# RWKV stage of a hybrid trunk: key transposes in another PSUM ring, the y split on another engine, a denser inverse

## The chip, the core and the metric

The kernel runs on one core of a Trainium2 chip. The metric is device time in microseconds (us) of one execution; lower is better. TensorE (PE) does the matrix products and transposes, VectorE (DVE), ScalarE (ACT) and GpSimd (POOL) the elementwise work, SyncE (SP) issues most of the transfers. Each engine takes its instructions strictly in order, so one that waits holds up all that stand behind it. TensorE's clock has two levels, 2.4 GHz (granted clock 1.0) and 1.2 GHz (0.5).

## The reference

One layer on 2048 tokens of width 1024. After a modulated RMS norm a projection feeds two halves of width 512, an RWKV-7 recurrence and a banded attention; both are gated, joined and projected out.

```python
def rwkv7_step(state, inp):
    r_t, w_t, k_t, v_t, a_t, b_t = inp
    sa = einsum('bhij,bhj->bhi', state, a_t)
    state = state * w_t + sa[..., None] * b_t + v_t[..., None] * k_t
    y = einsum('bhij,bhj->bhi', state, r_t)
    return state, y
...
y = group_norm(y) * lnx_g + lnx_b + sum(r * k * r_k) * v      # per head of 64
y = concat([y_r * silu(g_r), y_a * silu(g_a)])
x = x + gate * (y @ w_out)
```

## The kernel before

Phase A computes norm, projections and attention. The last stage, `phase_r`, runs the recurrence over 32 chunks of 64 tokens (`n` = 0 to 31), eight heads at once; four chunks make a block (`b` = 0 to 7, `c` = 0 to 3 inside it). Within a chunk the recurrence is a triangular system of 64 steps, so each chunk needs the inverse of a triangular matrix.

One chunk, in program order: `from_state` (products with the carried state `z`), `state_keys(n+1)` (PE turns the next chunk's keys, `ps_kt`, and ACT copies them to `kt`), `solve` (`ps_u`, then `uv`), `merge1` and `merge2` (they join the 32-wide inverses into 64-wide ones: `ps_mg`, `ps_mh`), `state` (`ps_z`; two DVE operations write the next `z`), `read_out` (`ps_py`, then `ys`), `qchunk(b+2)` (`ps_q`; DVE masks it into `g`), `from_values(n+1)`. Every second chunk `values` centres the values of a pair (`vf`, `ps_vr`), and the output of the pair before goes through `spread`, `scaled`, `flip` (transposes, `ps_yf`) and `gated` (two DVE operations on `yf`).

The inverse of a block's 32-wide pieces is DVE work alone: `inv(b+1)` has 31 steps of two operations (`pd`, then `xtt`), run during block `b`. When it is done SP writes it out (`xt_d`), reads it back into `g`, and DVE transposes it (`turn`, tile `x`). Only then can `merge1` of the next block's first chunk start; this stands at the end of the last chunk of a block, and is called the border below.

Between these pieces stands `gap()`: it lets one step of the output projection (`outputs`, three 512-wide products into `ps_out`) run on PE, and as many inverse steps on DVE as a rule on the number of calls asks for. The projection goes through 7 jobs of 32 steps. For its last four steps a job loads the next job's y (`yraw`), and `split_y` cuts it into a high part (`yh`, a cast on ACT) and a rest (`yl`, a subtraction). There is one `yh` and one `yl` tile for each quarter, so a cast waits for the last product that reads the tile.

The order on PE, DVE and ACT is the written one (`PINNED`); POOL and SP are ordered by the compiler's scheduler. Two PSUM rings have two buffers each. `psm` (tag `m`) holds `ps_kt`, `ps_mg`, `ps_vr`, `ps_yf` and `ps_q`; `ps_u` (tag `u`) holds `ps_u`, `ps_z` and `ps_mh`. A tile can be written when the tile two places before it in the ring has been read.

Of the kernel before, what the change touches and what calls it, by code (L numbers as in the profile page):

```python
# [9 lines left out]
F32 = mybir.dt.float32  # L10
# [8 lines left out]
P = 128  # L19
# [6 lines left out]
NP = 4  # L26
# [20 lines left out]
CS = {}  # L47
# [107 lines left out]
def q_setup(tc, nc, e, ra):  # L155
    eyes, pool, dp, C, ar_d, kb_d, y_d = (e[k] for k in ("eyes", "pool", "dp", "C", "ar_d", "kb_d", "y_d"))
    wo, xT, outT, psp, modv, split_half, gemm_k, sub = (e[k] for k in ("wo", "xT", "outT", "psp", "modv", "split_half", "gemm_k", "sub"))
    xa_d = dp.tile([KT, P, S], F32, name="xa_d")
    yr_d = dp.tile([NP, P, S], F32, name="yr_d")
    rq = pool("rq", e["ctx"], bufs=1, side="right", reuse_waits="tile")  # L160
# [97 lines left out]
            nc.gpsimd.dma_start(out=xa_d[m, :, tsl], in_=xt)  # L258
            yield

    return dict(xa_d=xa_d, yr_d=yr_d, y_d=y_d, rq=rq, ra=ra, prefetch=prefetch, st=blk_st, qchunk=qchunk, qmat=qmat, inv=inv, output=output, late=late)


def seq(*gs):
# [524 lines left out]
def phase_r(tc, nc, e, q_):  # L789
    C, col, ident = (e[k] for k in ("C", "col", "ident"))  # L790
    nhalf, pool, wcall, sub, gemm_k = (e[k] for k in ("nhalf", "pool", "wcall", "sub", "gemm_k"))
    bv_d, v_d, sg_d, wo, xT, cst, outT, wx, psp, modv = (e[k] for k in ("bv_d", "v_d", "sg_d", "wo", "xT", "cst", "outT", "wx", "psp", "modv"))
    xa_d, yr_d, y_d, rq, ra, blk_st = (q_[k] for k in ("xa_d", "yr_d", "y_d", "rq", "ra", "st"))
    NB, NCH = S // TR, S // 64
    LO, HI = slice(0, 64), slice(64, 128)
# [2 lines left out]
    with st:  # L798
# [9 lines left out]
        def load_pair(name, src, m):  # L808
            o = rp.tile([P, NP, P], F32, name=name, bufs=1)
            nc.sync.dma_start(out=o, in_=src[:, :, m * P:(m + 1) * P].rearrange("k p t -> p k t"))  # L810
            return o
# [5 lines left out]

        def state_keys(n):
            kb = of(n)[1]
            pk = psm("ps_kt")  # L820
            for p in range(NP):
                nc.tensor.transpose(pk[:, p * P:(p + 1) * P], kb[:, p].rearrange("p a b -> p (a b)"), ident)  # L822
            kts[n] = rp.tile([P, 8, 64], F32, name="kt", bufs=2)
            nc.scalar.copy(out=kts[n].rearrange("p a b -> p (a b)"), in_=pk)

        def values(n):
            vf = vfs.pop(n // 2)
            pv = psm("ps_vr")
            for p in range(NP):
                nc.tensor.matmul(pv[:, p * P:(p + 1) * P], lhsT=vf[:, p], rhs=cen, start=(p == 0), stop=(p == NP - 1))  # L830
            pv = pv.rearrange("p (a b) -> p a b", b=64)
            for d in range(2):
                uvs[n + d] = rp.tile([P, 8, 64], F32, name="uv", bufs=3)
                for q, (hr, _) in enumerate(HALVES):
                    nc.scalar.copy(out=uvs[n + d][hr, q::2, :], in_=pv[64 * d:64 * d + 64, q::2, :])
# [63 lines left out]
        def state(n, z):  # L899
            pz = ps_u.tile([P, NP, 64], F32, name="ps_z", tag="u")  # L900
            for i in range(NP):
                for q, (hr, _) in enumerate(HALVES):
                    nc.tensor.matmul(pz[hr, i, :], lhsT=kts[n][:, 2 * i + q, :], rhs=uvs[n][:, 2 * i + q, :], start=(i == 0), stop=(i == 3))
            zn = rp.tile([P, NP, 64], F32, name="z", tag="z", bufs=2)
            nc.vector.tensor_tensor(out=zn, in0=pz, in1=z, op=ALU.add)
            nc.vector.tensor_tensor(out=zn, in0=zn, in1=wcall[:, :, n].unsqueeze(2).broadcast_to([P, NP, 64]), op=ALU.mult)
            return zn

        def read_out(n, ys):
            g = of(n)[2]  # L910
            yr = slice(64 * (n % 2), 64 * (n % 2) + 64)
            for i in range(NP):
                for q, (hr, _) in enumerate(HALVES):
                    nc.tensor.matmul(pys[n][q][hr, i, :], lhsT=g[:, 2 * i + q, 0:64], rhs=uvs[n][:, 2 * i + q, :],
                                     start=False, stop=(i == 3))
            for q, (hr, _) in enumerate(HALVES):
                nc.scalar.copy(out=ys[yr, q::2, :], in_=pys[n][q][hr])

        def square(ys):
            ysq = rp.tile([P, 8, 64], F32, name="ysq", bufs=1)  # L920
            nc.scalar.activation(ysq, ys, AF.Square)
            return ysq
# [12 lines left out]
        def flip(ys):  # L935
            pf = psm("ps_yf")
            for p in range(NP):
                nc.tensor.transpose(pf[:, p * P:(p + 1) * P], ys[:, 2 * p:2 * p + 2, :].rearrange("p a b -> p (a b)"), ident)
            yf = rp.tile([P, NP, P], F32, name="yf", bufs=2)
            for p in range(NP):  # L940
                nc.scalar.activation(yf[:, p, :], pf[:, p * P:(p + 1) * P], AF.Identity, scale=col("lg", p), bias=col("lb", p))
            return yf
# [36 lines left out]
        def split_y(r, k):  # L979
            n = r.shape[1]  # L980
            hi, lo = (ra.tile([P, 512], F32R, name=f"{t}{k}", bufs=1)[:, 0:n] for t in ("yh", "yl"))
            nc.scalar.copy(out=hi, in_=r)
            sub(nc.gpsimd, lo, r, hi)
            return hi.unsqueeze(1), lo.unsqueeze(1)

        def outputs(jobs, fin):
# [40 lines left out]
        fill = outputs(jobs, False)  # L1027
        work = dict(inv=iter(()), calls=0, done=0)

        def gap():  # L1030
            next(fill, None)
            work["calls"] += 1
            want = min(32, max(0, 9 * (work["calls"] - 4) // 4))
            while work["done"] < want:
                next(work["inv"], None)
                work["done"] += 1

        cen = rp.tile([P, P], F32, name="cen", bufs=1)
        nc.sync.dma_start(out=cen, in_=cst[:, CS["cen"][0]:CS["cen"][1]])
        with tc.manual_schedule(engines=PINNED):  # L1040
            z = rp.tile([P, NP, 64], F32, name="z", tag="z", bufs=2)
            nc.gpsimd.memset(z, 0.0)
            vfs[0] = load_pair("vf", v_d, 0)
            for m in range(2):
                load_w(m, 1)
            load_sides(0)
            turn(0)
            state_keys(0)
            merge1(0)
            values(0)  # L1050
            merge2(0)
            gap()
            from_values(0)
            pend = None
            for n in range(NCH):
                b, c = divmod(n, NCB)
                even, more, border = n % 2 == 0, n + 1 < NCH, n % NCB == NCB - 1
                if c == 0:
                    if b + 2 < NB:
                        q_["prefetch"](b + 2)  # L1060
                    work.update(inv=q_["inv"](b + 1) if b + 1 < NB else iter(()), calls=0, done=0)
                    next(work["inv"], None)
                pb = from_state(n, z)
                if more:
                    state_keys(n + 1)
                gap()
                solve(n, pb)
                if more and not border:
                    merge1(n + 1)
                if even and more:  # L1070
                    vfs[n // 2 + 1] = load_pair("vf", v_d, n // 2 + 1) if n + 2 < NCH else None
                if even and pend is not None:
                    scaled(*pend[1:])
                gap()
                gap()
                yf = None
                if even and pend is not None:
                    yf = flip(pend[1])
                elif not even and more:
                    values(n + 1)  # L1080
                zn = state(n, z)
                if even:
                    ys = rp.tile([P, 8, 64], F32, name="ys", bufs=1)
                read_out(n, ys)
                z = zn
                if not even:
                    ysq = square(ys)
                gap()
                if yf is not None:
                    gated(pend[0], yf)  # L1090
                    load_sides(n // 2)
                gap()
                if more and border:
                    turn(b + 1)
                    merge1(n + 1)
                gap()
                if more:
                    merge2(n + 1)
                if not even:
                    pend = n // 2, ys, spread(ysq)  # L1100
                if b + 2 < NB:
                    q_["qchunk"](b + 2, c, psm)
                if more:
                    from_values(n + 1)
            for _ in range(12):
                next(fill, None)
            scaled(*pend[1:])
            yf = flip(pend[1])
            drain(fill)
            gated(pend[0], yf)  # L1110
            drain(outputs([(3, 0, 256, 256)], True))
# [44 lines left out]
```

## Time and profile before

| | |
|---|---|
| median of three runs | 1775.95 us (1772.7 to 1777.89) |
| profiled execution | 1771.38 us, of which the span is 1769.6 us |
| mean granted clock | 0.951 |
| DMA traffic | 231.6 MB |

The span counts from the first to the last instruction of the program. All times of day below are us from its start. The RWKV stage takes the stretch from about 1265 to 1770.

### The profile page before, as it was taken

To read this page: it belongs to the slowest core of one execution; us is meant where nothing else is said; L and a number is where in the kernel's file an instruction comes from. 1 tells how busy PE (TensorE), PEld (TensorE's weight loads), DVE (VectorE), ACT (ScalarE), POOL (GpSimd) and SP (SyncE) were. 2 spreads that over 40 slices of the span, in tenths; PEclk is the share of its full clock that TensorE was granted. 3 is DMA by queue.
4 is the path that set the end of the run, shared out by engine and by line. 5 is a ranking of instruction groups with operands and counts; after the bars stand their busy time and mean duration, and the time that the engine had idled before them with its cause. 6 is when DMAs were issued, how large, how long until landed. Compare 5 with 4: busy or idle time off the path is not lost. (4 is left out here: it accounts for less than half of the span.)

```text
span 1769.6 us, 32130 instructions
## 1 busy us (share of the span) xinstructions
PE 1553.7 (88%) x11944; PEld 1270.9 (72%) x11944; DVE 1090.2 (62%) x2407; ACT 929.9 (53%) x2087; POOL 708.4 (40%) x571
## 2 busy tenths in 40 slices
PE   3899998899999899999979999978688889889795
PEld 2677876678777678888868878856576667767685
DVE  7647457475576846746566574576555576566732
ACT  3666556566555565656566666652234344444440
POOL 4455544555444455444536544505212121221221
PEclk9999999899999999999999999999788999899897
DMA  8463333332324523223142332255746665664532
GB/s 286 130 222 102 100 114 101 114 119 73 113 93 135 167 72 125 81 93 114 60 137 72 126 102 66 66 192 159 229 129 183 167 195 154 187 183 122 148 115 90
DMA packets 188957, 231.60 MB, mean 131 GB/s; under 512 B 62976, under 2 KB 101632, under 8 KB 188800
## 3 DMA queue, kind: packets, MB, share of 16 engines
q1 hardware_dynamic: 183552, 212.76, 39.6%
q0 software_dynamic: 5248, 16.78, 2.7%
q8 instruction: 94, 1.54, 0.4%
q14 instruction: 63, 0.52, 0.1%
HBM read 171.30 MB, written 58.20 MB: 130 GB/s over the span
## 5 line engine op out<-in xcount | busy, mean ns | idle before, releaser
L111 POOL TENSOR_TENSOR wlo<-raw,whi 128x512 fp32r<-128x512 f32 x272 | 369.9, 1364 | 424.4 <-ACT whi L122 374.9
L122 ACT CAST whi<-raw 128x512 fp32r<-128x512 f32 x272 | 167.6, 618 | 173.9 <-issue 53.5
L130 PE MATMUL ps_r<-hh,whi 128*128 128x512 f32 x544 | 219.5, 404 | 13.8 <-ACT carry L632 10.6
L132 PE MATMUL ps_r<-hh,wlo 128*128 128x512 f32 x544 | 218.1, 401 | 2.2 <-POOL wlo L111 2.2
L131 PE MATMUL ps_r<-hl,whi 128*128 128x512 f32 x544 | 218.1, 401 | 0.0
L130 PE MATMUL ps_qkvg<-hh,whi 128*128 128x512 f32 x480 | 196.0, 410 | 10.7 <-ACT carry L632 7.1
L131 PE MATMUL ps_qkvg<-hl,whi 128*128 128x512 f32 x480 | 194.4, 406 | 9.0 <-DVE hl L377 5.3
L132 PE MATMUL ps_qkvg<-hh,wlo 128*128 128x512 f32 x480 | 192.7, 402 | 0.4 <-POOL wlo L111 0.4
L111 DVE TENSOR_TENSOR ptl<-ps_pt,pth 128x384 fp32r<-128x384 f32 (+1 forms) x232 | 105.2, 473 | 43.5 <-ACT pth L598 42.9
L130 PEld LDWEIGHTS ps_r<-hh,whi 128*128 128x128 f32 x544 | 103.5, 190 | 34.8 <-ACT carry L632 11.4
L588 ACT ACTIVATE sp<-sp,mn 128x640 f32<-128x640 f32 (+4 forms) x128 | 97.9, 765 | 53.9 <-DVE mn L584 53.0
L132 PEld LDWEIGHTS ps_r<-hh,wlo 128*128 128x128 f32 x544 | 103.3, 190 | 24.8 <-POOL wlo L111 3.1
L131 PEld LDWEIGHTS ps_r<-hl,whi 128*128 128x128 f32 x544 | 103.5, 190 | 20.1
L130 PEld LDWEIGHTS ps_qkvg<-hh,whi 128*128 128x128 f32 x480 | 92.0, 192 | 32.8 <-ACT carry L632 8.5
L131 PEld LDWEIGHTS ps_qkvg<-hl,whi 128*128 128x128 f32 x480 | 91.9, 191 | 31.1 <-DVE hl L377 7.5
L598 ACT CAST pth<-ps_pt 128x384 fp32r<-128x384 f32 (+1 forms) x232 | 90.8, 416 | 42.8 <-PE ps_pt L595 39.9
L132 PEld LDWEIGHTS ps_qkvg<-hh,wlo 128*128 128x128 f32 x480 | 92.2, 192 | 21.0 <-POOL wlo L111 0.6
L595 PE MATMUL ps_pt<-cs,sp 128*128 128x128 f32 x560 | 94.5, 281 | 10.8 <-DVE ptl L111 4.3
L604 PE MATMUL ps_o<-ptl,vc 128*128 128x256 f32 x336 | 92.5, 301 | 9.5 <-DVE ptl L111 9.5
L603 PE MATMUL ps_o<-pth,vc 128*128 128x256 f32 x336 | 92.2, 295 | 8.2 <-ACT pth L598 5.9
L1019 POOL DMA_DIRECT2D out<-xres x40 | 22.3, 557 | 173.3 <-DVE xres L1018 131.6
L582 DVE CUSTOM_DVE_ANT_0 sp<-ps_sa,mab 128x384 f32<-128x384 f32 (+1 forms) x112 | 58.7, 524 | 43.4 <-PE ps_sa L558 26.8
(256 smaller groups left out, 3713.5 us busy)
## 6 DMA issues: line engine op xcount, KB each, us to landing
raw<-in_wi SPq DMA_DIRECT2D x264, 256.0 KB, 2.9
hx<-in_xT SPq DMA_DIRECT2D x32, 256.0 KB, 5.4
wada<-in_wadaT SPq DMA_DIRECT2D x16, 512.0 KB, 8.7
ar_d<-art SPq DMA_DIRECT2D x16, 512.0 KB, 3.7
kb_d<-kbt SPq DMA_DIRECT2D x16, 512.0 KB, 3.2
kb<-kb_d SPq DMA_DIRECT2D x8, 1024.0 KB, 5.9
ar<-ar_d SPq DMA_DIRECT2D x8, 1024.0 KB, 6.4
xres<-in_xT SPq DMA_DIRECT2D x32, 256.0 KB, 3.4
```

Of the source, the lines that this page charges most:

```text
L111: eng.tensor_tensor(out=out, in0=full, in1=hi.bitcast(F32), op=ALU.subtract)
L122: nc.scalar.copy(out=hi, in_=raw)
L130: nc.tensor.matmul(ps, lhsT=wh[:, f], rhs=hh[:, k, :], start=first, stop=False)
L131: nc.tensor.matmul(ps, lhsT=wh[:, f], rhs=hl[:, k, :], start=False, stop=False)
L132: nc.tensor.matmul(ps, lhsT=wl[:, f], rhs=hh[:, k, :], start=False, stop=last)
L582: nc.vector.tensor_tensor_reduce(out=sp[:, 0:na], in0=sa[:, 0:na], in1=m_ap, scale=1.0, scalar=3e38, op0=ALU.add, op1=ALU.min, accum_out=m ...
L588: nc.scalar.activation(sp[:, 0:n], sp[:, 0:n], AF.Exp, scale=-1.0, bias=mn[:, 1:2], accum_out=ls[:, 2 * v + hh_:2 * v + hh_ + 1])
L595: nc.tensor.transpose(pp[:, kk - lo, :], sp[:, kk * P:(kk + 1) * P], ident)
L598: nc.scalar.copy(out=ph, in_=pp)
L603: nc.tensor.matmul(po[:, hh_, :], lhsT=wv_, rhs=pth[:, m, :], start=(m == m0), stop=False)
L604: nc.tensor.matmul(po[:, hh_, :], lhsT=wv_, rhs=ptl[:, m, :], start=False, stop=(m == 5))
L1019: nc.gpsimd.dma_start(out=dst[m, :, tsl], in_=xt)
```

## The change

- `state_keys` writes `ps_kt` into the ring `u` in place of the ring `m`. The ring `u` now serves `ps_kt`, `ps_u` twice, `ps_z` and `ps_mh` twice.
- `split_y` subtracts on DVE in place of POOL (28 tiles over the stage, 24 of 512 columns and 4 of 256).
- The inverse's rule becomes 5/2 steps per call after the fourth, from 9/4. The last of the six calls in a chunk moves behind `qchunk`.
- In a chunk: `scaled` moves behind one more `gap`; `state` and `read_out` come ahead of `flip` and `values`; `gated` comes behind two gaps; `qchunk` comes ahead of `spread`. `ys` gets two buffers, `yf` one.
- The first `vf` and `cen` live in the pool `rq`, and are loaded at the end of phase A.
- 15 in place of 12 projection steps run ahead of the last `scaled`.

```diff
+    cen = rq.tile([P, P], F32, name="cen", bufs=1)
+    nc.sync.dma_start(out=cen, in_=cst[:, CS["cen"][0]:CS["cen"][1]])
+    vf0 = load_vf(0)
...
         def state_keys(n):
             kb = of(n)[1]
-            pk = psm("ps_kt")
+            pk = ps_u.tile([P, 512], F32, name="ps_kt", tag="u")
...
-            sub(nc.gpsimd, lo, r, hi)
+            sub(nc.vector, lo, r, hi)
...
-        def gap():
+        def gap(steps=True):
             next(fill, None)
+            if steps:
+                invert()
+        def invert():
             work["calls"] += 1
-            want = min(32, max(0, 9 * (work["calls"] - 4) // 4))
+            want = min(32, max(0, 5 * (work["calls"] - 4) // 2))
...
+                gap()
                 if even and pend is not None:
                     scaled(*pend[1:])
                 gap()
-                gap()
-                yf = None
+                zn = state(n, z)
+                if even:
+                    ys = rp.tile([P, 8, 64], F32, name="ys", bufs=2)
+                read_out(n, ys)
+                z = zn
                 if even and pend is not None:
                     yf = flip(pend[1])
-                elif not even and more:
-                    values(n + 1)
-                zn = state(n, z)
-                if even:
-                    ys = rp.tile([P, 8, 64], F32, name="ys", bufs=1)
-                read_out(n, ys)
-                z = zn
                 if not even:
                     ysq = square(ys)
+                    if more:
+                        values(n + 1)
                 gap()
-                if yf is not None:
+                gap()
+                if even and pend is not None:
                     gated(pend[0], yf)
                     load_sides(n // 2)
-                gap()
                 if more and border:
                     turn(b + 1)
                     merge1(n + 1)
-                gap()
+                gap(False)
                 if more:
                     merge2(n + 1)
+                if b + 2 < NB:
+                    q_["qchunk"](b + 2, c, psm)
+                invert()
                 if not even:
                     pend = n // 2, ys, spread(ysq)
-                if b + 2 < NB:
-                    q_["qchunk"](b + 2, c, psm)
```

What stands on DVE in the third chunk of block 5, where the inverse ends (no split falls there). Before:

```order
L905 TENSOR_TENSOR z<-ps_z,z 128x256
L906 TENSOR_TENSOR z<-z,wcall 128x256
L1018 SCALAR_TENSOR_TENSOR xres<-ps_out,modv,xres 128x512
L228 TENSOR_TENSOR pd<-xtt,lt 128x91
L230 TENSOR_TENSOR xtt<-xtt,pd 128x13x7
L228 TENSOR_TENSOR pd<-xtt,lt 128x78
L230 TENSOR_TENSOR xtt<-xtt,pd 128x13x6
L228 TENSOR_TENSOR pd<-xtt,lt 128x70
L230 TENSOR_TENSOR xtt<-xtt,pd 128x14x5
L946 TENSOR_TENSOR yf<-yf,bv 128x512
L947 SCALAR_TENSOR_TENSOR yf<-yf,gg 128x512
L228 TENSOR_TENSOR pd<-xtt,lt 128x56
```

Now, from the same operation on `z` on:

```order
L914 TENSOR_TENSOR z<-ps_z,z 128x256
L915 TENSOR_TENSOR z<-z,wcall 128x256
L1027 SCALAR_TENSOR_TENSOR xres<-ps_out,modv,xres 128x512
L229 TENSOR_TENSOR pd<-xtt,lt 128x56
L231 TENSOR_TENSOR xtt<-xtt,pd 128x14x4
L229 TENSOR_TENSOR pd<-xtt,lt 128x45
L231 TENSOR_TENSOR xtt<-xtt,pd 128x15x3
L229 TENSOR_TENSOR pd<-xtt,lt 128x30
L231 TENSOR_TENSOR xtt<-xtt,pd 128x15x2
L229 TENSOR_TENSOR pd<-xtt,lt 128x16
L231 TENSOR_TENSOR xtt<-xtt,pd 128x16
L955 TENSOR_TENSOR yf<-yf,bv 128x512
```

The two `yf` operations (`gated`) have moved from inside the inverse to behind its end, and three more inverse steps stand ahead of `z`.

At the start of the stage, on ACT, with the semaphores that each instruction waits for (DMAHW: a transfer's). Before:

```order
L824 COPY kt<-ps_kt 128x512 [waits DMAHW5_49,DVE_49,PE_49]
L857 COPY mg<-ps_mg_12639 32x4x32 [waits PE_49,Pool_49]
L857 COPY mg<-ps_mg_12640 32x4x32 [waits PE_49]
L835 COPY uv<-ps_vr 64x4x64 [waits DMAHW4_49,PE_49,Activation_49]
L835 COPY uv<-ps_vr 64x4x64 x3
```

Now:

```order
L833 COPY kt<-ps_kt 128x512 [waits PE_49]
L866 COPY mg<-ps_mg_12639 32x4x32 [waits PE_49,Pool_49]
L866 COPY mg<-ps_mg_12640 32x4x32 [waits PE_49]
L844 COPY uv<-ps_vr 64x4x64 [waits DVE_49,DMAHW7_49,PE_49,Activation_49]
L844 COPY uv<-ps_vr 64x4x64
```

The order is the same; the wait for a transfer has moved from the first copy of keys to the first copy of values.

## Rows read from the trace of the kernel before

**Rows 1.** The page's first line.
```profile
span 1769.6 us, 32130 instructions
```

**Rows 2.** Waits, 1282 to 1707 us: who waited for whom, us in total, times, longest.
```profile
PE ps_kt L822 <- DVE g L205: 32.9, 14, 4.3
...
PE ps_mg L853 <- DVE x L846: 13.4, 6, 6.0
...
PE ps_mg L853 <- DMA g<-xt_d: 8.5, 6, 3.1
...
PEld ps_u L895 <- ACT kt L824: 7.7, 17, 0.7
```

**Rows 3.** Windows from an inverse's first operation to its last: blocks 0, 4, 6; sum of seven.
```profile
core 0: us, PE busy (x) PEld busy (x) DVE busy (x) ACT busy (x) POOL busy (x), PEclk, DMA share, GB/s
1294.38:1329.84 35.46, 28.86 (x418) 23.79 (x414) 25.72 (x83) 13.91 (x38) 3.92 (x5) 0.86 0.40 129
...
1534.25:1561.29 27.04, 25.07 (x424) 20.98 (x422) 23.93 (x80) 11.83 (x34) 3.35 (x4) 1.00 0.65 196
...
1639.15:1667.67 28.52, 23.68 (x358) 19.14 (x356) 25.85 (x75) 14.80 (x39) 8.86 (x8) 0.88 0.48 143
sum 209.05, PE 176.65 PEld 145.77 DVE 178.16 ACT 91.81 POOL 37.20; mean PE 25.24 PEld 20.82 DVE 25.45 ACT 13.12 POOL 5.31
```

**Rows 4.** Windows from an inverse's end to the transpose after it: first, last, sum of seven.
```profile
1329.84:1338.05 8.21, 7.57 (x72) 6.24 (x73) 3.39 (x7) 3.33 (x9) 0.54 (x1) 0.79 0.73 174
...
1667.67:1678.37 10.70, 5.42 (x62) 4.29 (x58) 1.52 (x5) 3.56 (x9) 0.54 (x1) 0.92 0.69 158
sum 68.59, PE 51.65 PEld 40.75 DVE 22.07 ACT 33.39 POOL 8.16; mean PE 7.38 PEld 5.82 DVE 3.15 ACT 4.77 POOL 1.17
```

**Rows 5.** Windows from that transpose to the next inverse's first operation: two of six, sum.
```profile
1398.66:1415.60 16.94, 15.56 (x194) 12.65 (x195) 7.41 (x13) 5.62 (x17) 2.81 (x3) 0.80 0.71 192
...
1570.00:1587.90 17.90, 15.64 (x269) 12.92 (x269) 11.28 (x13) 8.62 (x24) 6.52 (x6) 1.00 0.80 214
...
sum 106.35, PE 95.83 PEld 78.13 DVE 53.05 ACT 42.15 POOL 25.39; mean PE 15.97 PEld 13.02 DVE 8.84 ACT 7.02 POOL 4.23
```

**Rows 6.** Timeline of DVE, 1577 to 1597 us: start, us, engine, line.
```profile
1581.24 0.42 DVE L905 TENSOR_TENSOR z<-ps_z,z 128x256 f32<-128x256 f32 x1 [4.49 <-PE ps_z L903]
...
1583.42 4.56 DVE L947 SCALAR_TENSOR_TENSOR yf<-yf,gg 128x512 f32<-128x512 f32 x1
1587.90 0.18 DVE L228 TENSOR_TENSOR pd<-xtt,lt 128x31 f32<-128x31 f32 x1
```

**Rows 7.** The same stretch on POOL.
```profile
1583.71 3.71 POOL L111 TENSOR_TENSOR yl<-yraw,yh 128x512 fp32r<-128x512 f32 x3
```

**Rows 8.** Groups by line, 1290 to 1700 us: busy us, mean ns of one, idle before.
```profile
L111 POOL TENSOR_TENSOR yl<-yraw,yh 128x512 fp32r<-128x512 f32 x20 | 26.2, 1326 | 26.7 <-ACT yh L982 26.6
...
L946 DVE TENSOR_TENSOR yf<-yf,bv 128x512 f32<-128x512 f32 x14 | 9.6, 683 | 0.0
...
L111 DVE TENSOR_TENSOR wrl<-raw,wrh 128x512 fp32r<-128x512 f32 x10 | 7.0, 705 | 16.3 <-ACT wrh L969 13.8 <-PE ps_yf L938 2.5
```

**Rows 9.** Timeline at the start of the stage, 1268 to 1283 us, ACT and PE.
```profile
1271.06 0.59 ACT L824 COPY kt<-ps_kt 128x512 f32<-128x512 f32 x1 [9.04 <-DMA bv_d<-r]
...
1271.69 1.06 PE L853 MATMUL ps_mg<-x,g 64*64 64x32 f32 x14 [4.42 <-ACT kt L824]
...
1276.44 2.05 PE L830 MATMUL ps_vr<-cen,vf 128*128 128x128 f32 x8 [3.69 <-DMA vf<-v_d]
...
1278.57 1.50 ACT L835 COPY uv<-ps_vr 64x256 f32<-64x256 f32 x4 [5.38 <-issue]
...
1281.07 0.80 PE L130 MATMUL ps_out<-yh,whi 128*128 128x512 f32 x1 [1.58 <-ACT yh L982]
```

**Rows 10.** The chain that ended last, ahead of a border.
```profile
1562.60 5.10 DMA xt_d<-xtt
```

**Rows 11.** Timeline of the tail on PE, 1722 to 1770 us.
```profile
1728.78 1.12 PE L938 MATMUL ps_yf<-cs,ys 128*128 128x128 f32 x4 [2.86 <-DVE ys L933]
```

More of the change, by code (lines that the diff above doesn't have):

```diff
@@ L157, in q_setup @@
     wo, xT, outT, psp, modv, split_half, gemm_k, sub = (e[k] for k in ("wo", "xT", "outT", "psp", "modv", "split_half", "gemm_k", "sub"))
+    v_d, cst = e["v_d"], e["cst"]
     xa_d = dp.tile([KT, P, S], F32, name="xa_d")
@@ L259, in output, with load_vf @@
             yield
-    return dict(xa_d=xa_d, yr_d=yr_d, y_d=y_d, rq=rq, ra=ra, prefetch=prefetch, st=blk_st, qchunk=qchunk, qmat=qmat, inv=inv, output=output, late=late)
+    def load_vf(m):
+        o = rq.tile([P, NP, P], F32, name="vf", bufs=1)
+        nc.sync.dma_start(out=o, in_=v_d[:, :, m * P:(m + 1) * P].rearrange("k p t -> p k t"))
+        return o
+    cen = rq.tile([P, P], F32, name="cen", bufs=1)
+    nc.sync.dma_start(out=cen, in_=cst[:, CS["cen"][0]:CS["cen"][1]])
+    vf0 = load_vf(0)
+    return dict(cen=cen, vf0=vf0, load_vf=load_vf, xa_d=xa_d, yr_d=yr_d, y_d=y_d, rq=rq, ra=ra, prefetch=prefetch, st=blk_st, qchunk=qchunk, qmat=qmat, inv=inv, output=output, late=late)
 def seq(*gs):
@@ L791, in phase_r @@
     nhalf, pool, wcall, sub, gemm_k = (e[k] for k in ("nhalf", "pool", "wcall", "sub", "gemm_k"))
-    bv_d, v_d, sg_d, wo, xT, cst, outT, wx, psp, modv = (e[k] for k in ("bv_d", "v_d", "sg_d", "wo", "xT", "cst", "outT", "wx", "psp", "modv"))
+    bv_d, sg_d, wo, xT, outT, wx, psp, modv = (e[k] for k in ("bv_d", "sg_d", "wo", "xT", "outT", "wx", "psp", "modv"))
     xa_d, yr_d, y_d, rq, ra, blk_st = (q_[k] for k in ("xa_d", "yr_d", "y_d", "rq", "ra", "st"))
@@ L938, in flip @@
                 nc.tensor.transpose(pf[:, p * P:(p + 1) * P], ys[:, 2 * p:2 * p + 2, :].rearrange("p a b -> p (a b)"), ident)
-            yf = rp.tile([P, NP, P], F32, name="yf", bufs=2)
+            yf = rp.tile([P, NP, P], F32, name="yf", bufs=1)
             for p in range(NP):
@@ L1036, in gap @@
                 work["done"] += 1
-        cen = rp.tile([P, P], F32, name="cen", bufs=1)
-        nc.sync.dma_start(out=cen, in_=cst[:, CS["cen"][0]:CS["cen"][1]])
+        cen, load_vf = q_["cen"], q_["load_vf"]
         with tc.manual_schedule(engines=PINNED):
@@ L1042, in phase_r @@
             nc.gpsimd.memset(z, 0.0)
-            vfs[0] = load_pair("vf", v_d, 0)
+            vfs[0] = q_["vf0"]
             for m in range(2):
@@ L1070, in phase_r @@
                 if even and more:
-                    vfs[n // 2 + 1] = load_pair("vf", v_d, n // 2 + 1) if n + 2 < NCH else None
+                    vfs[n // 2 + 1] = load_vf(n // 2 + 1) if n + 2 < NCH else None
+                gap()
                 if even and pend is not None:
@@ L1095, in phase_r @@
                     merge1(n + 1)
-                gap()
+                gap(False)
                 if more:
                     merge2(n + 1)
+                if b + 2 < NB:
+                    q_["qchunk"](b + 2, c, psm)
+                invert()
                 if not even:
                     pend = n // 2, ys, spread(ysq)
-                if b + 2 < NB:
-                    q_["qchunk"](b + 2, c, psm)
                 if more:
                     from_values(n + 1)
-            for _ in range(12):
+            for _ in range(15):
                 next(fill, None)
```

## Prediction

> **What bounds the kernel now.** I read the page first: the span is 1769.6 us [rows 1], the profiled execution 1771.38 us, 1.8 us more. The change touches the RWKV stage alone, so I went on to the waits inside it. PE's largest idle time there is `ps_kt` waiting for DVE's mask `g`, 32.9 us in 14 waits; the waits at the borders come to some 22 us, 13.4 behind the transpose and 8.5 behind the transfer ahead of it [rows 2]. Read so, the stage is PE's, and the change takes 33 us out of it. That is not how I read it.
>
> The third view cuts the stage at DVE's inverse. From an inverse's first operation to its last, DVE is busy 178.16 of 209.05 us in seven stretches; in block 4, where no split falls, the stretch is 27.04 us, DVE works 23.93 of it, and most of what is left is the gap of some 0.04 us between its 80 operations [rows 3]. So in a stretch DVE has no room. From the inverse's end to the transpose (SP writes it out, reads it back) it takes 68.59 us in seven, at best about 8.1; the write alone takes 5.10 us to land [rows 4, 10]. From the transpose to the next inverse's start it is 106.35 us in six [rows 5]; PE works nearly all of that (15.56 of 16.94). These three follow one upon the other without a hole: inverse on DVE, transfer, PE's way to the next `z`, inverse. Their sum, 384.0 us from 1294.4 to 1678.4, is the loop. A PE wait inside the first part is free time that the part has anyway. The reader is to see that the wait for `g` is DVE being late, and taking the keys out of the ring doesn't make DVE earlier.
>
> **The change, part by part.**
>
> *Keys in ring u.* The 14 waits vanish where they stand. DVE's work remains, and what is late next is `z` (wanted by `merge2` and `from_state`), the mask (wanted by `merge1`), or the border. I count 0 for it, with bounds 0 and -32.9 plus what the clock gives back. The second `ps_u` now waits for ACT's copy of the keys, in the ring's next place. Weight loads for `ps_u` already end 17 waits on that copy, 7.7 us in all [rows 2], and PE's products do not show there, so projection products cover it; bounds 0 and +7.7, I take 0.
>
> *gated and flip.* Without splits, DVE goes from `z` through one `xres` and the two `yf` operations to the inverse. The two cost 2 x 0.683 = 1.4 us [rows 8]. Now the first inverse steps stand ahead of them, and `state` stands ahead of `flip` (1.12 us for its transposes at the lower clock [rows 11], so some 0.5 at the higher, an estimate). The inverse starts 1.9 us sooner after the border in the four of six stretches without a split: -7.5. At its end the two operations of the pair's next turn leave the stretch, so its length stays 27.0: one enters, one leaves. The denser rule then matters little: DVE has no idle time for it to use, it only puts three more steps ahead of `z`. That can hurt when PE wants `z`; PE has a good 3 us of projection, readout and masks ahead of the first use, which cover three steps of two operations (23.93 us over 80 operations is 0.3 each [rows 3], so 1.8 us).
>
> *The y split on DVE.* In the row of block 5 the second `yf` operation takes 4.56 us where the `yf` operation ahead of it takes 0.683 in the mean, while POOL runs three splits of 3.71 us [rows 6, 7]. So when DVE has work, a split on POOL (1326 ns) costs DVE nearly its whole length, and one on DVE costs what the like split of a weight costs, 705 ns [rows 8]. For 24 splits of 512 columns that is 24 x 0.6 = 14 us to gain at most; less, since not all fall where DVE is full.
>
> The Trainium skill, "Perfetto Trace Analysis", section "Optimizing Scalar/DVE Operations", says that with DVE saturated, work may be moved to other engines, though between GpSimd and DVE that "might not help", because they share a read port under an exclusive lock. The row agrees with the lock and goes beyond the rest: the move to POOL was dearer than doing the work on DVE. By the rule that a full DVE is to be spared, the splits would add 24 x 0.705 = 16.9 us; that is weighed among the rivals.
>
> A split on DVE has a new wait: ACT's cast, which waits for PE's last product with the old tile and for what ACT has ahead. The weight splits idled DVE for 13.8 us over ten [rows 8]. Where DVE is behind, the wait is hidden. It isn't in blocks 1 and 5, where two splits now stand between `z` and the inverse: ACT has two copies, the four activations of `flip` (1.5 us, as four copies take [rows 9]) and two casts ahead. I estimate 5.9 us from `z` to the first step, where the row has 1581.24 to 1587.90, 6.66 [rows 6]; with the flip -1.3 in each of the two, -2.6.
>
> *Lengths of the seven stretches after.* Seven times 27.0 is 189. Blocks 0 and 3 hold three weight splits each (2.1 and about 0.9 of waiting): +6.0. Blocks 1 and 5 hold two y splits: +1.9 each with some waiting, +3.8. Block 2 holds four: +3.3. Block 6 holds four but no masks: +0.5. Sum 202.6, so -6.4 against 209.05 [rows 3]; most of it is block 0, 35.46 at a granted clock of 0.86, which had PE late.
>
> *Inverse end to transpose.* The sum is 11.1 us over seven times the first, 8.21 [rows 4]. Part of it is transfer, part a transpose standing behind a weight split that came late because PE was. I take -4.5; bounds 0 and -11.1.
>
> *First values.* At the start ACT's copy of the first keys waits 9.04 us for the store `bv_d<-r`, whose place in SBUF it takes, until 1271.06; `ps_mg` waits 4.42 us for the copy, `ps_vr` 3.69 us for the load of `vf`, and the first projection product 1.58 us, until 1281.07 [rows 9]. Now `vf` is there, and the wait for a transfer has moved to the first copy of values, which I take to be the same store, ended at 1271.06. From that copy's start to the product it was 1278.57 to 1281.07, 2.5 us; so it starts at 1273.6: -7.5. Bounds: -3.7 (only the load's wait) and -9.7 (all three).
>
> *Tail.* The last `flip` waits 2.86 us for `scaled` [rows 11]; three more projection steps (some 1 us for products of half width) and POOL without splits ahead of the `pow` and the stores take a part: -2, bounds 0 and -3. The last 16 loads of `xres` each wait for an earlier store, which stays.
>
> *Clock.* Borders stay, and since PE is no longer held at the keys it gets there earlier and waits longer. The stretch after a border ran at 0.80 [rows 5], between 1.2 and 2.4 GHz. I add +2 for it.
>
> *Moved with no price:* `values` and `square` behind `read_out` (ACT's copies are wanted only by `from_values`, behind two or three projection steps); `scaled` one step later (its reader, `flip`, is later too); the second `ys` buffer (`flip` now reads the old one behind the write of the new); one `yf` buffer (its store has a pair of chunks, over 20 us). Were the cover of `scaled` gone, it would cost as the 2.86 us in the tail.
>
> Sum: -7.5 - 2.6 - 6.4 - 4.5 - 7.5 - 2 + 2 = -28.5, so 1742.9 for an execution like the profiled one. The median of the three runs, 1775.95, stands 4.6 above that one. I take half of this: **1745**.
>
> **The rivals.**
>
> *PE's path after all.* If DVE catches up wherever PE runs, the 32.9 us are gained in full, with the start and the tail and about 10 us from the clock (an estimate: block 0's stretch ran at 0.86 [rows 3], so 28% of its 35.46 us at the lower level, some 5 us lost; twice that for the loop). For it: in block 4's stretch PE is busy 25.07 of 27.04 us [rows 3], so the two engines are nearly even. Against: shortening PE's side of an even pair gains nothing. 1771.4 - 52 = about 1719, with half the offset 1721.
>
> *The splits are no relief.* By the page's rule as a mechanism here: DVE's queue is the bound, and what POOL's splits blocked was time in which DVE would have waited. Then the blocks in 1, 5, 2 and 6 (3.9 + 3.9, and some 3.7 each) come back as no gain: +15, 1760. For it: DVE is not busy in 3.11 of block 4's 27.04 us [rows 3]. Against: 4.56 us for one operation, directly ahead of an inverse [rows 6].
>
> *Slower: DVE stands at the splits.* In order, DVE holds `z` and the inverse behind a split that waits for a cast. If DVE reaches each of the 24 wide splits before its cast is done, each costs 0.7 us and the wait of a weight split, 13.8 us over ten [rows 8], together 2.1; 24 of them are 50 us, of which the forecast counts some 12. That is 38 more, 1783. It decides where DVE has no backlog when a split comes up; the full stretches say it has.
>
> **How the numbers follow.** Forecast 0.70, own range 1730 to 1757; PE's path 0.12 (1710 to 1730); no relief 0.11 (1757 to 1768); slower or no change 0.07 (1768 to 1790). The bounds of the border term (-6.6 to +4.5), the start (-2.2 to +3.8) and the ring (up to +7.7) fill the forecast's range. Leaving out about 0.1 on each side gives 1725 to 1762. Within 0.3% (5.3 us), which is about what a measurement of this kernel can tell, counts as the same: faster 0.91, same 0.05, slower 0.04.
>
> **What would show it.** No waits of `ps_kt` for DVE; in their place longer waits of `ps_mg` for the transpose, `ps_mh` or `ps_py` for `z`. Inverse stretches of 27 to 30 us, summing to some 203. No `yf` or `pd` over 1 us. The first projection product of the stage near 1273.6. Wrong: stretches below 26 us (then PE set them), or DVE idle for casts of y by more than 10 us in total.

## Result, and the profile after

Median 1752.61 us (1748.91 to 1759.35), against 1776.24 for the kernel before beside it; ratio 0.987, 95% interval 0.9838 to 0.9902. The time lies in the predicted range, 7.6 us above the forecast. The profiled execution took 1749.66 us.

The page's first line, beside [rows 1]:
```profile
span 1747.9 us, 32132 instructions
```
The waits of the changed kernel, 1282 to 1707 us, beside [rows 2]:
```profile
PE ps_mg L862 <- DVE x L855: 12.8, 6, 3.8
PE ps_yf L947 <- DVE ys L942: 11.2, 3, 4.9
PE ps_yf L947 <- DVE pd L229: 10.2, 4, 2.9
PE ps_mg L862 <- DMA g<-xt_d: 3.6, 3, 2.6
PE ps_mg L862 <- DVE g L206: 3.0, 9, 0.6
```
`ps_kt` no longer waits for the mask. In its place stands `ps_yf`, 21.4 us in seven where before has one wait of 4.8: in the third chunk of every block the flip waits for `scaled` (four of the seven are put down to the `pd` that starts as `scaled` ends). The windows of the inverse, beside [rows 3]:
```profile
1286.99:1317.03 30.04, 26.30 (x389) 21.58 (x386) 24.54 (x81) 13.29 (x36) 3.89 (x5) 0.94 0.42 136
...
1514.35:1540.93 26.58, 24.97 (x378) 20.30 (x378) 23.94 (x79) 12.40 (x36) 3.93 (x5) 1.00 0.58 184
...
1623.89:1649.53 25.64, 19.67 (x264) 15.59 (x265) 23.68 (x79) 12.46 (x32) 3.66 (x4) 0.93 0.45 139
sum 193.06, PE 166.51 PEld 134.43 DVE 173.67 ACT 88.53 POOL 26.48; mean PE 23.79 PEld 19.20 DVE 24.81 ACT 12.65 POOL 3.78
```
From the inverse's end to the transpose, beside [rows 4]:
```profile
1317.03:1326.56 9.53, 8.09 (x111) 6.30 (x107) 4.58 (x8) 5.30 (x13) 0.54 (x1) 1.00 0.92 209
...
1649.53:1659.38 9.85, 8.49 (x131) 6.72 (x125) 2.91 (x5) 5.29 (x14) 0.54 (x1) 1.00 0.87 203
sum 73.64, PE 63.48 PEld 50.73 DVE 33.28 ACT 38.75 POOL 3.78; mean PE 9.07 PEld 7.25 DVE 4.75 ACT 5.54 POOL 0.54
```
From the transpose to the next inverse, all six:
```profile
1326.56:1346.62 20.06, 18.79 (x235) 15.51 (x237) 7.50 (x13) 7.90 (x22) 2.42 (x3) 0.74 0.63 176
1383.05:1399.12 16.07, 14.73 (x187) 12.14 (x188) 6.29 (x12) 5.31 (x17) 2.64 (x3) 0.79 0.67 195
1439.37:1456.09 16.72, 15.50 (x185) 12.87 (x186) 6.82 (x13) 5.61 (x16) 2.20 (x2) 0.69 0.64 190
1497.77:1514.35 16.58, 15.36 (x185) 12.80 (x186) 6.29 (x11) 4.99 (x15) 2.22 (x3) 0.69 0.52 143
1551.68:1570.65 18.97, 17.60 (x243) 14.47 (x245) 7.58 (x14) 7.79 (x22) 2.66 (x3) 0.82 0.60 167
1606.60:1623.89 17.29, 16.22 (x265) 13.06 (x264) 6.30 (x12) 8.53 (x26) 2.80 (x3) 1.00 0.59 142
sum 105.69, PE 98.19 PEld 80.85 DVE 40.78 ACT 40.12 POOL 14.95; mean PE 16.37 PEld 13.47 DVE 6.80 ACT 6.69 POOL 2.49
```
and, of the same windows of the kernel before, the four that [rows 5] leave out:
```profile
1338.05:1360.56 22.51, 19.69 (x274) 15.91 (x272) 11.29 (x13) 10.02 (x27) 6.52 (x6) 0.85 0.64 181
...
1456.72:1473.72 17.00, 15.66 (x197) 12.73 (x198) 8.13 (x15) 6.24 (x18) 2.81 (x3) 0.80 0.70 203
1517.27:1534.25 16.98, 15.63 (x194) 12.68 (x195) 7.44 (x14) 5.62 (x17) 3.93 (x4) 0.80 0.52 140
...
1624.13:1639.15 15.02, 13.64 (x239) 11.23 (x242) 7.50 (x13) 6.04 (x19) 2.81 (x3) 1.00 0.65 164
```
The start on ACT and PE, beside [rows 9]:
```profile
1264.22 0.59 ACT L833 COPY kt<-ps_kt 128x512 f32<-128x512 f32 x1 [3.16 <-PE ps_b L724]
...
1272.18 1.50 ACT L844 COPY uv<-ps_vr 64x256 f32<-64x256 f32 x4 [3.60 <-DMA bv_d<-r]
...
1274.68 0.80 PE L130 MATMUL ps_out<-yh,whi 128*128 128x512 f32 x1 [3.25 <-ACT yh L991]
```
The spans differ by 21.7 us. To the first inverse -7.4 (1286.99 against 1294.38), the seven stretches of the inverse -16.0, six times from its end to the transpose +5.9 (73.64 less the last, 9.85, against 68.59 less 10.70), six from there to the next inverse -0.7, behind the last inverse -3.5 (98.4 against 101.9).

### The profile page after: what moved, and what is told of

It reads as the page before. It is cut to its first block, busy times and chain, and to the rows that moved or that the text cites. A ratio compares the mean times of both kernels' runs of the same rounds, so it can differ in the third digit from the quotient of the medians.

```text
span 1747.9 us, 32132 instructions
## 1 busy us (share of the span) xinstructions
PE 1557.5 (89%) x11944; PEld 1272.7 (73%) x11944; DVE 1086.2 (62%) x2435; ACT 929.7 (53%) x2087; POOL 675.5 (39%) x543
## 4 chain that ended last, share of the span: by engine, by line
PE 57%; DVE 21%; DMA 8%; issue 6%; ACT 5%; POOL 1%; SPq 1%; POOLq 0%; DVEq 0%; ACTq 0%
PE ps_qkvg L130 6%; PE ps_qkvg L131 6%; PE ps_qkvg L132 6%; PE ps_r L130 5%; PE ps_r L131 5%; PE ps_r L132 5%; DVE xtt L231 3%; DVE pd L229 3%; PE ps_pt L604 2%; DVE kbt L318 2%; PE ps_o L613 2%; PE ps_out L130 2%; PE ps_o L612 2%; DMA g<-xt_d 1%; PE ps_out L131 1%
## 5 line engine op out<-in xcount | busy, mean ns | idle before, releaser
L130 PE MATMUL ps_r<-hh,whi 128*128 128x512 f32 x544 | 220.4, 405 | 13.4 <-ACT carry L641 10.1
```

The costliest lines, as they stand in the source:

```text
L130: nc.tensor.matmul(ps, lhsT=wh[:, f], rhs=hh[:, k, :], start=first, stop=False)
```

## The experiments

Medians of 4 to 10 executions that spread over up to some 20 us; ratios are to the kernel before, with their 95% intervals. Two kernels whose intervals overlap are told apart here by their traces or not at all.

**One part alone, on the kernel before.** Ring u (`a1`):
```diff
-            pk = psm("ps_kt")
+            pk = ps_u.tile([P, 512], F32, name="ps_kt", tag="u")
```


> The kernel before with one edit: the keys' product in ring u. Theory A (the loop is the inverse on DVE, the transfer, and PE's way to the next inverse; a wait of PE inside an inverse costs nothing by itself): the 14 waits of ps_kt for the mask are gone, waits for z or the border grow by as much, the seven inverse stretches stay near 209 us, and the time moves by 0 to -5 us. Rival B (PE's path is what counts): the waits' 32.9 us come back for the most part, -15 us or more, with stretches shorter by about 4 us each.

1769.52 us, 0.9959 (0.9936 to 0.9982). The keys' wait went to the border and `merge1` as theory A says (`ps_mg` for the transfer 21.7 us, where [rows 2] has 8.5; for the mask 10.6). But the stretches fell to 202.3 and the median by 7, a little more than A allows and far less than B. So A is half right: DVE got `z` sooner (its waits for `ps_z` inside the stretches are 4.6 us, before 7.2) and its idle time there fell from 30.9 to 25.5; but the times to the next inverse rose from 106.4 to 114.2.

The y split (`a2`):
```diff
-            sub(nc.gpsimd, lo, r, hi)
+            sub(nc.vector, lo, r, hi)
```


> The kernel before with one edit: the 24 splits of y on DVE instead of POOL. Theory A: yf and inverse operations of over 1 us are gone, the inverse stretches of blocks 0, 2, 3, 5 and 6 shorten, and the time falls by 6 to 12 us. Rival C (what POOL's splits blocked was time in which DVE would have waited): within 3 us of no change. Rival D (DVE stands at the splits until ACT's casts are done): slower by 5 us or more, with DVE waits for yh of over 15 us in total.

1777.27 us, 1.0005 (0.998 to 1.003): nothing, as rival C says. Its windows of the inverse, all seven:
```profile
sum 212.58, PE 179.20 PEld 147.37 DVE 175.27 ACT 92.00 POOL 24.29; mean PE 25.60 PEld 21.05 DVE 25.04 ACT 13.14 POOL 3.47
```
and a row of its waits, 1282 to 1700 us:
```profile
DVE yl L111 <- ACT yh L982: 26.0, 8, 14.4
```
DVE is busy 2.9 us less in the stretches than before and idle 6.4 more (212.58 - 175.27 = 37.3; before 209.05 - 178.16 = 30.9 [rows 3]). What POOL's splits blocked was there to be saved, but DVE then stood at its casts: 6.4 of the 26.0 us of waits for `yh` lie inside the stretches (14.4 more are one wait ahead of the first). That is rival D's sign (over 15 us) without its price.

The first values and the centring matrix loaded in `q_setup` (`a3`):
```diff
-            vfs[0] = load_pair("vf", v_d, 0)
+            vfs[0] = q_["vf0"]
```


> The kernel before with one edit: the centring matrix and the first values are loaded in the tail of the stage ahead. Theory A and its rivals agree here: the first projection product of the stage comes about 7.5 us earlier than 1281.07 and everything behind it is moved by as much, -7.5 us. If it gives nothing, the 7.4 us by which the changed kernel enters its first inverse earlier came from the order at the start.

1767.54 us, 0.9956 (0.9921 to 0.999). The median moved as forecast, yet in the profiled execution the product came at 1281.70. That execution reached the stage late; counted from one DVE instruction of the stage ahead (last section), the product comes after 148.3 us where before takes 153.5.

**The order without ring and split** (`a4`: the changed kernel with both of those edits undone; the denser rule and the early first values are in it).

> The changed kernel with the keys back in the general ring and the splits of y back on POOL: what is left is the order (scaled, flip, gated, values, inverse steps) and the early first values. Theory A: the flip now waits for the scaled output behind denser inverse steps, about 3 us in each block, and the order gives next to nothing; -7.5 us from the first values and 0 to -4 from the order, so -7 to -12 against before. Rival E (the order is what made the inverse stretches shorter): -15 us or more, with stretches summing below 200 us.

1758.22 us, 0.9887 (0.9846 to 0.9929): rival E. The flip's waits are there (17.7 us) and don't prevent it. Its windows of the inverse, all seven:
```profile
sum 196.93, PE 165.90 PEld 135.51 DVE 179.13 ACT 89.35 POOL 40.03; mean PE 23.70 PEld 19.36 DVE 25.59 ACT 12.76 POOL 5.72
```
DVE's idle time in them is 17.8 us where before has 30.9. The cause shows in DVE's wait for `ps_z`, 1282 to 1700 us, in the kernel before:
```profile
DVE z L905 <- PE ps_z L903: 66.3, 21, 7.4
```
and in the changed one:
```profile
DVE z L914 <- PE ps_z L912: 38.9, 14, 6.3
```
It is 34.4 us here, and 56.4 and 63.5 with ring or split alone. Inside the stretches it falls to nothing: no wait for `ps_z` in `a4` or the changed kernel, 7.2 us in all before, the longest in block 0:
```profile
1322.05 0.42 DVE L905 TENSOR_TENSOR z<-ps_z,z 128x256 f32<-128x256 f32 x1 [4.22 <-PE ps_z L903]
```
So in the new order DVE gets `z` sooner. That `state` ahead of `flip` and `values` does it is the likely reading; this move was not run apart from the others.

**One part undone or moved, in the changed kernel.** `scaled` back ahead of the second gap (`b1`):
```diff
+                if even and pend is not None:
+                    scaled(*pend[1:])
                 gap()
-                if even and pend is not None:
-                    scaled(*pend[1:])
```


> The changed kernel with scaled back ahead of the second gap. In the changed kernel the flip waits for the scaled output in the third chunk of every block, 1.5 to 4.9 us each, 21.3 us in seven. Theory F (PE's way is late by this wait, and the time from the inverse's end to the transpose, which grew by 5 us, pays for it): the seven waits fall below 1 us each and the time falls by 6 to 15 us against the changed kernel, to about 1738 to 1747. Rival G (DVE is the bound, so PE only waits elsewhere): waits of ps_mg or ps_mh grow by as much as the flip's vanish, within 3 us of the changed kernel.

1757.7 us, 0.989 (0.9857 to 0.9922): no gain; the median is 5.1 above the changed kernel's, more than G's 3, but the intervals overlap. The flip's waits fell by half, to 11.8 us, and `ps_mg`'s wait for the transpose rose from 12.8 to 23.3, as rival G says.

The flip one gap later (`b2`):
```diff
-                if even and pend is not None:
-                    yf = flip(pend[1])
...
                 gap()
+                if even and pend is not None:
+                    yf = flip(pend[1])
                 gap()
```


> The changed kernel with the flip one gap later, behind a projection step, so that PE has a step of work while DVE scales. Theory F: the flip's waits fall from 21.3 us to about 8 and the time by 4 to 10 us against the changed kernel; the pair gated, which needs the flip's copies on ACT, then stands closer behind it and may take some of this back (DVE waiting for yf). Rival G: within 3 us of the changed kernel.

1751.49 us, 0.9851 (0.9808 to 0.9894). In the trace theory F's 7 us are there (waits 14.2, the first inverse's start to the last one's end 355.4 where the changed kernel has 362.5); the median doesn't show them. Open.

The y split on POOL again, the edit of `a2` undone (`b3`):

> The changed kernel with one part undone: the splits of y back on POOL. In the stretches of the inverse of the changed kernel twelve splits on DVE cost some 8 us, and the inverse's own operations are 8.9 us shorter than before, so by theory C' (what DVE takes over it pays in full) this stays within 4 us of the changed kernel, with inverse operations of 118 to 123 us in sum instead of 110.4. By the prediction's step (the splits are the relief) it is slower by 8 us or more.

1759.45 us, 0.9899 (0.9865 to 0.9933): 6.8 above the changed kernel, between the two expectations. Its windows of the inverse, all seven:
```profile
sum 197.16, PE 165.98 PEld 134.85 DVE 178.70 ACT 89.14 POOL 41.44; mean PE 23.71 PEld 19.26 DVE 25.53 ACT 12.73 POOL 5.92
```
DVE is busy 5.0 us more than with the split on DVE, and idle for 18.5 where the changed kernel has 19.4. So in this order 4.1 of the 5.0 us count; in the old one (`a2`) the relief turned into idle time. The medians' intervals overlap: the traces show it, the medians alone don't.

The keys in the general ring again, the edit of `a1` undone (`b4`):

> The changed kernel with one part undone: the keys' product back in the general ring. The two parts ring and split together were worth 5.6 us on top of order and first values. Theory C' (the split gives nothing): it is slower than the changed kernel by 4 to 8 us, with ps_kt waiting for the mask again by 15 to 20 us. By the prediction's step (the ring gives nothing): within 3 us of the changed kernel.

1752.28 us, 0.9865 (0.9825 to 0.9905): the same as the changed kernel, though `ps_kt` waits 17.0 us for the mask again. The prediction's step holds here; theory C' falls.

The old rule (`b5`):
```diff
-            want = min(32, max(0, 5 * (work["calls"] - 4) // 2))
+            want = min(32, max(0, 9 * (work["calls"] - 4) // 4))
```


> The changed kernel with one part undone: the inverse's steps by the old rule (nine steps to four calls). The prediction gave the denser rule nothing, since DVE has no idle time for it. Theory N (prediction): within 3 us of the changed kernel, the flip's waits a little shorter. Rival R (the denser rule ends the inverse one or two gaps earlier and is what made the stretches of the inverse shorter by the 12 us that the order brought): stretches sum to 200 us or more and the median is slower by 6 us or more.

1765.42 us, 0.9932 (0.991 to 0.9955), 12.8 above the changed kernel and still below the kernel before; the intervals of the two changed kernels don't touch: rival R. Its windows of the inverse, all seven:
```profile
sum 208.31, PE 189.67 PEld 154.40 DVE 189.01 ACT 100.32 POOL 25.89; mean PE 27.10 PEld 22.06 DVE 27.00 ACT 14.33 POOL 3.70
```
Idle is 19.3 us, as in the changed kernel; DVE is busy 15.3 us more. By the old rule the last two steps of a stretch stand behind `gated` and the third chunk's two masks, which so lie inside it: six masks and four `yf` operations in a full stretch, where the changed kernel has four and two.

**The rule alone** (`e1`: the kernel before with the edit of `b5` the other way round).

> The kernel before with one edit: the denser rule (five steps to two calls). Theory S (it is where the inverse's last steps stand on DVE that counts: in the kernel before they already stand ahead of the third chunk's masks, so the rule alone takes nothing out of the stretch): the seven stretches sum to 205 us or more, within 4 us of the kernel before. Theory B (steps issued earlier are a backlog that covers DVE's waits for z and for ACT's casts, 30.9 us of idle time in the stretches before and 19.4 in the changed kernel): idle time below 24 us, stretches below 202 us, and faster by 6 us or more. By either, the flip waits longer in the third chunks.

1794.02 us, 1.0092 (1.0069 to 1.0115): slower by 16.8. Its windows of the inverse, all seven:
```profile
sum 213.52, PE 176.00 PEld 144.25 DVE 178.37 ACT 87.80 POOL 37.23; mean PE 25.14 PEld 20.61 DVE 25.48 ACT 12.54 POOL 5.32
```
Idle is 35.2 us, and DVE waits 58.9 for `ps_z` in the loop: nothing of theory B, and S for the stretches, though 4.5 us longer is a little past its 4. What S left out is that the two other times grew too, from 68.6 and 106.4 to 77.3 and 117.9 us in sum. What made them grow isn't settled; the clock may be part of it (0.76 to 0.82 in all six windows ahead of an inverse, where two of before have 1.00).

**`gated` and its loads behind the border** (`c1`), and with `b2`'s later flip (`c2`):
```diff
-                if even and pend is not None:
+                if c == 0 and pend is not None:
                     gated(pend[0], yf)
                     load_sides(n // 2)
+                if c == 2:
+                    held = pend[0], yf, n // 2
                 if more and border:
                     turn(b + 1)
                     merge1(n + 1)
+                if border:
+                    gated(*held[:2])
+                    load_sides(held[2])
```
The reason stands in SP's timeline of the changed kernel at the end of an inverse:
```profile
1373.46 1.27 SPq L234 DMA_DIRECT2D xt_d<-xtt  x2
1374.82 0.67 SPq L819 DMA_DIRECT2D bv<-bv_d  x1
1375.59 1.62 SPq L959 DMA_DIRECT2D yr_d<-yf  x1
1377.26 0.50 SPq L819 DMA_DIRECT2D gg<-sg_d  x1
1377.85 0.49 SPq L1012 DMA_DIRECT2D xres<-in_xT  x1
1378.61 2.33 SPq L237 DMA_DIRECT2D g<-xt_d  x4
```


> The changed kernel with gated and load_sides of a block's third chunk moved behind the border's transpose and first merge. In the changed kernel the store of yf and the loads of gg and bv stand on SP between the inverse's write and its reading back; the four reads land in 5.1 us where they took 2.3 before. Theory T (the transfer got slower because these 768 KB now run beside it, and the 5 us by which the seven times from the inverse's end to the transpose grew come from there): the reads land in 2.5 to 3.5 us, the seven times sum to 58 to 66 us instead of 73.6, and the median falls by 5 to 12 us against the changed kernel's 1752.6. Rival P (PE is behind at the inverse's end, because of the flip's waits, and the border waits for PE's own work): the seven times fall by less than 3 us and the median by less than 3 us.

1750.0 us, 0.9847 (0.9815 to 0.988). The mechanism is right: the reads land in 2.9 us, and the seven times sum to 64.1. The DMA issues, 1290 to 1690 us (KB each, median us to landing), of the kernel before:
```profile
xt_d<-xtt SPq DMA_DIRECT2D x14, 128.0 KB, 5.0
g<-xt_d SPq DMA_DIRECT2D x28, 64.0 KB, 2.3
```
of the changed one:
```profile
xt_d<-xtt SPq DMA_DIRECT2D x14, 128.0 KB, 3.2
g<-xt_d SPq DMA_DIRECT2D x28, 64.0 KB, 5.1
```
of `c1`:
```profile
g<-xt_d SPq DMA_DIRECT2D x28, 64.0 KB, 2.9
```
The write `xt_d` shows the other side of the same thing: landing took 5.0 us before, when such transfers were issued just ahead of it (at one border from 1386.23 to 1388.01, the write at 1388.70), and takes 3.2 now that they come behind it. With the old rule (`b5`), where `gated` stands inside the inverse again, the write takes 5.3 and the reads 2.3, and the seven times sum to 62.6. So the move sped up the write and slowed down the reads by more.

But in `c1` the time to the next inverse grew from 105.7 to 113.4 us, so the median fell by 2.6 only, which isn't told apart from nothing: theory T is right about the transfer and wrong about the gain.

> The run before this one with the flip one gap later too. In the run with the later flip alone, the flip's waits fell by 7.1 us and the stretch from the first inverse to the last end by 7.1 us, though its median fell by 1.1 only. Theory F (those 7 us are real and the median was hit by executions that came late to the stage): another 4 to 8 us below the run with gated late. Rival: within 3 us of it.

1748.72 us, 0.9844 (0.9816 to 0.9872), the rival: within 3 us of `c1`. The two sums are 60.2 and 119.0. What is late next is the inverse's own input, by the waits of `c2`, 1282 to 1690 us:
```profile
DVE pd L229 <- DMA lt<-l_d: 18.1, 3, 9.6
```
Its load stands on SP behind an `xres` load that waits for its buffer. That this is the next limit was not tested. `c1` and `c2` beat the kernel before; against the changed kernel they aren't resolved.

## Why the prediction came out

The forecast of a gain of 28.5 us met 21.7 in the spans, with three terms far off: the stretches of the inverse gave 9.6 us more than forecast, the times from its end to the transpose 9.6 less, and those to the next inverse, with the clock's term, 7.4 less. That the total came so near is in part luck, since the first two cancel.

- **Start, -7.5: right.** The product came 6.4 us earlier. Counted from the same instruction of the stage ahead, it comes after 147.0 to 149.9 us in the ten kernels with early values and after 153.5 to 156.3 in the four without: -6.6 in the mean (in these two kernels 153.5 and 148.3). ACT's first copy of values waits for `bv_d<-r` as forecast.
- **Inverse stretches, -6.4: mis-sized, -16.0.** DVE is busy 4.5 us less (178.16 to 173.67) and idle 11.5 less (30.9 to 19.4). The busy part comes with the split (179.13 and 178.70 in `a4` and `b3`, which split on POOL), the idle part with the order. The step that failed is "in a stretch DVE has no room": I read the idle time as the gaps between operations, and from block 4, where 1.1 of 3.11 us are waits. In all seven DVE waited 7.2 us for `z`, 7.7 at the weight splits and 1.6 for products of the projection; in the changed kernel 0, 3.5 and 0, with 2.1 new for masks. The new order removed the waits for `z`: none in `a4` and `b5` (17.8 and 19.3 idle), 4.6 to 11.3 us in the four kernels without it (`a1`, `a2`, `a3`, `e1`). The forecast gave the earlier `state` one flip's length at the border alone.
- **"The denser rule then matters little": wrong.** The changed kernel without it is 12.8 us slower (`b5`); the rule without the order makes the kernel before 16.8 slower (`e1`). "One enters, one leaves" holds only with both.
- **The split, "14 us to gain at most", and its rival: each right in one order.** On the kernel before it gives nothing (`a2`), in the changed one about 7 us by medians whose intervals overlap, 4.1 of it in the stretches (`b3`). The Trainium skill, "Perfetto Trace Analysis", section "Optimizing Scalar/DVE Operations", doubts that moving work from DVE to GpSimd helps. The trace goes further: with the split on POOL DVE is busy 5.0 us more in the stretches than when it does the split itself (`b3`).
- **Keys in ring u, 0: right in the changed kernel** (`b4`), not on the kernel before, where they gave 7 us (`a1`). The bounds held it. "Taking the keys out of the ring doesn't make DVE earlier" is too strong there: in `a1` DVE's waits for `z` inside the stretches fell by 2.6 us.
- **Transpose to next inverse, -7.5 and -2.6: -0.7; clock, +2: perhaps some +10.** Weighted by granted clock, the six windows fall from 92.8 (22.51 x 0.85 + 16.94 x 0.80 + 17.00 x 0.80 + 16.98 x 0.80 + 17.90 + 15.02) to 83.4 (20.06 x 0.74 + 16.07 x 0.79 + 16.72 x 0.69 + 16.58 x 0.69 + 18.97 x 0.82 + 17.29): -9.4. If the clock sets these windows, the work fell about as forecast, and the mean clock's fall from 0.873 to 0.789, more time at 1.2 instead of 2.4 GHz, ate it (83.4 / 0.873 would be 95.5, 10.2 less than 105.7). In the five low windows PE begins with a wait of 2.0 to 3.8 us at the border, in the one at 1.00 with 0.6 and 0.5; before, a window at 1.00 began with 2.3 us of waits. The rows don't all bear it out: the window at 1.00 took 17.29 us, more than three of the low ones, with 265 operations on PE where they have 185 to 187, and in `c1`, where `gated` has come into them, three windows at 1.00 took 17.40 to 20.26. That the clock is the cause is worked out from the windows, not tested by a run, and how much of the 10 us is its doing stays open.
- **Inverse end to transpose, -4.5: wrong sign, +5.1.** I followed SP up to the inverse's write and not past it. With the inverse ending ahead of `gated`, a store and three loads of 256 KB each run between the write and the reads: the reads land in 5.1 us in place of 2.3, the write in 3.2 in place of 5.0 (`c1`, `b5`). The result lies outside the bounds of 0 and -11.1.
- **`scaled` at no price: the wait came, the price didn't.** The flip's waits are 21.4 us, and taking half of them away moved as much to the border (`b1`), as the prediction's opening argues of a PE wait inside the inverse. That such waits are free in general is not shown: in the trace of `b2` 7 us less of them went with a loop 7 us shorter.
- **Tail, -2:** -3.5 behind the last inverse, 0.9 of it the last transfer.

Of the signs, the keys' waits are gone, no `yf` or `pd` in the loop takes over 1 us, and the first product came at 1274.68, 1.1 us past the forecast. `ps_mg`'s waits for the transpose did not grow (12.8, before 13.4). Both signs of being wrong came up, each by a little. The last stretch took 25.64 us, below 26, though PE, busy for 19.67 of it, did not set it. And DVE's wait for casts of y came to 10.5 us in five (1282 to 1700 us), over the bound of 10. All of it lies outside the inverse: 3.1 us ahead of block 3's transpose (12.97 us after its inverse's end, the longest), 2.4 in each of two stretches ahead of the next inverse, 2.7 behind the last transpose.

## What to carry to other kernels

Price a reordering by listing what stands on the busy engine's queue between the first and the last step of the critical chain, and follow the transfer queue through the chain's own write and read back. Work taken off an engine may count only once that engine no longer waits inside the chain: here the same edit was worth nothing in one order and some 7 us in the other. Before reading an engine as full, add up what it waits for inside the critical stretch, over all stretches and not the cleanest one. A wait taken from the engine with slack may come back at the next place, and a link made shorter may lengthen the next one.

## What the hardware showed

Kernels that are alike up to the RWKV stage reach it at different times. One DVE instruction of the stage ahead, from DVE's timeline of the changed kernel:
```profile
1126.41 0.74 DVE L639 SCALAR_TENSOR_TENSOR k<-ps_r,sct,k 128x511 f32<-128x511 f32 x1
```
and of `b2`:
```profile
1134.47 0.74 DVE L639 SCALAR_TENSOR_TENSOR k<-ps_r,sct,k 128x511 f32<-128x511 f32 x1
```
It starts at 1125.4 to 1134.8 us in the fourteen profiled executions. The loop differs as well where the program in it is nearly the same (`a3`, in which `vf` and `cen` lie in another pool): from the first inverse's start to the last one's end 373.3 us before, 380.6 in `a3`. So differences of a few us between single spans say little; for what lies ahead of the loop, times counted from a common instruction say more.
